# Source order on every engine, and weights' pieces issued three ahead from a flat list, in a two-layer decoder trunk

## The chip, the core and the metric

The kernel runs on one core of one Trainium2 chip. The core has engines that run their own instruction queues side by side: TensorE (PE) multiplies matrices and transposes, VectorE (DVE) and ScalarE (ACT) work elementwise, GpSimd (POOL) does what is left, and SyncE (SP) issues most transfers. An engine begins an instruction when the semaphores on which it waits have come. The metric is the device time of one execution in microseconds (us).

## What is computed

The input is x, 256 tokens of 2048 features in float32. Two layers follow each other, each a norm, one wide projection, a mixer, one output projection and a residual sum.

```python
def even_mixer(h, w_in, conv_w, w_out, pos):        # w_in: 2048 x 8192
    proj = h @ w_in
    q, k, v, g_ret, gate_b, gate_c, u, g_conv = jnp.split(proj, 8, axis=-1)
    ...
    o = retention_chunkwise(q, k, v.reshape(shp))
    ret_out = rms_norm_nogain(o).reshape(b, s, RET_WIDTH) * jax.nn.silu(g_ret)
    ...
    conv_out = gate_b * conv * jax.nn.silu(g_conv)
    return jnp.concatenate([ret_out, conv_out], axis=-1) @ w_out

def odd_mixer(h, w_in, q_norm_w, k_norm_w, sinks, w_out, pos):   # w_in: 2048 x 4608
    proj = h @ w_in
    q, k, v, gate = jnp.split(proj, [ATTN_WIDTH, ATTN_WIDTH + KV_WIDTH, ATTN_WIDTH + 2 * KV_WIDTH], axis=-1)
    q = rope(rms_norm(q.reshape(b, s, ATTN_Q_HEADS, ATTN_HEAD_DIM), q_norm_w), pos)
    k = rope(rms_norm(k.reshape(b, s, ATTN_KV_HEADS, ATTN_HEAD_DIM), k_norm_w), pos)
    o = swa_sinks(q, k, v, sinks).reshape(b, s, ATTN_WIDTH)
    return (o * jax.nn.silu(gate)) @ w_out
```

The attention of the odd layer has 32 query heads and 4 key heads of width 64, a window of 128 keys, and a learned sink per head in the softmax's divisor.

## The kernel before

**Products.** Every projection is computed as three products of rounded halves: x and w are each split into a high part and a remainder, and high times high, high times low and low times high are added. A projection goes in **chunks** of 512 output columns (`Chunk`, L126). A chunk has eight **pieces** of two k-tiles; the piece's weights are one transfer of 512 KB into `raw`, a copy on ACT that rounds them to `wh` (L165), and a subtraction on DVE that leaves `wl` (L166). These three are called the **split** (L157). `raw`, `wh` and `wl` have five buffers each. A piece's twelve matmuls (L143) go into two PSUM tiles, one for each half of the tokens (t = 0 and 1). Transfers, copies and subtractions are named for the chunk: `whog_3` is the rounded piece 3 of a gate chunk, `wloq_6` the remainder of piece 6 of a query chunk.

**Stages.** Layer 0 has sixteen chunks (names `e`), then four for its output projection (`eo`). The odd layer has nine: keys and values (`kv`), then q0, g0, q1, g1, q2, g2, q3, g3, where q is a chunk of eight query heads and g the gate of the same heads; then four chunks of output projection (`oo`). `stage` (L169) runs the first two chunks of a stage in turns, six pieces of the first, six of the second, two and two; the rest run one by one. When a chunk ends, its `done` function reads its PSUM tiles: `kv` (L516), `queries` (L566) or `gate` (L556).

**Side work.** What follows a chunk is partly put into generators in `pending`, and `feed` (L132) takes one step of them behind each piece (L136). `keys_values` (L525) scales and splits the keys, then transposes them on PE into two buffers of the pool `tp`, from which ACT copies them to kT (L551). `attention` (L589) runs through two chunks: it transposes the split queries (qt, L598, copied to q1T), computes scores for two heads at a time, masks them (L612 to L621), takes the shift and the sink (L625 to L636), the exponentials (L641), the divisor (L646), multiplies the gate with it (`scale_gate`, L654), transposes probabilities (pt) and the gate (gt, L665), computes values (ov, L697) and gates them (`gated`, L699). `finish` (L747) splits the result into the activations a2h and a2l of the last projection. `queries` needs, for each half of the tokens, a Square on ACT, a string of steps on DVE (a reduction, a product, two half products, a sum and a short step), and two copies qs on ACT.

**Order.** The program is written as one thread of calls, but the framework orders each engine's queue when it builds the program: an instruction may be moved ahead of others that stand earlier in the source, where its buffers are free. Splits have been moved up to five pieces ahead of their matmuls in this way, as far as the five buffers go.

Of the kernel before, what the change touches and what calls it, by code (L numbers as in the profile page):

```python
# [8 lines left out]
F32 = mybir.dt.float32  # L9
F32R = mybir.dt.float32r  # L10
AF = mybir.ActivationFunctionType
ALU = mybir.AluOpType
# [3 lines left out]
P = 128  # L16
# [4 lines left out]
N = 512  # L21
PK = 2
NP = KT // PK
# [7 lines left out]
EVEN_ORDER = [4, 0, 2, 6, 5, 1, 3, 7, 10, 12, 14, 8, 11, 13, 15, 9]  # L31

ODD_COLS = [2048, 0, 2560, 512, 3072, 1024, 3584, 1536, 4096]
ODD_KIND = [("kv", 0)] + [(k, i) for i in range(4) for k in ("q", "g")]

RAW_BUFS, HL_BUFS, W2_BUFS, WARM, LAST = 5, 5, 5, 2, 3


C_ID = 0
# [14 lines left out]
S_END = S_SINK + 32  # L54


@with_exitstack
def hybrid_kernel(
    ctx: ExitStack,
# [9 lines left out]
    const1: bass.AP,  # L69
    out: bass.AP,  # L70
):
    nc = tc.nc

    cp = ctx.enter_context(tc.tile_pool(name="cp", bufs=1))
    wp = ctx.enter_context(tc.tile_pool(name="wp", bufs=1))
# [14 lines left out]
    def f32(a):  # L90
        return a.bitcast(F32)

    class Act:


        def __init__(self, name):
            self.name, self.groups = name, []
# [15 lines left out]
    def step(n=1):  # L113
        while n and pending:
            try:
                next(pending[0])
                n -= 1
            except StopIteration:
                pending.popleft()

    def drain():
        while pending:
            step()


    class Chunk:  # L126
# [5 lines left out]
        def feed(self, lo, hi, steps=1, fine=False, late=False):  # L132

            for pc in range(lo, hi):
                self.products(pc, *self.split(pc, fine), late=late)
                step(steps)  # L136

        def products(self, pc, wh, wl, ts=range(T), late=False):

            def product(k, t, a, w):  # L140
                kt = pc * PK + k
                self.n[t] += 1
                nc.tensor.matmul(  # L143
                    self.ps[t], self.act(kt)[a][:, t * P : (t + 1) * P], w[:, k * N : (k + 1) * N],
                    start=self.n[t] == 1, stop=self.n[t] == 3 * KT,
                )

            for a, w in ((0, wh), (1, wh), (0, wl)) if late else ():
                for k in range(PK):
                    for t in ts:  # L150
                        product(k, t, a, w)
            for k in range(0 if late else PK):
                for t in ts:
                    for a, w in ((0, wh), (0, wl), (1, wh)):
                        product(k, t, a, w)

        def split(self, pc, fine=False):  # L157
            nm = f"{self.name}_{pc}"
            raw = wp.tile([P, PK * N], F32, tag="raw", name=f"w{nm}", bufs=RAW_BUFS)
            wh = wp.tile([P, PK * N], F32R, tag="wh", name=f"wh{nm}", bufs=HL_BUFS)  # L160
            wl = wp.tile([P, PK * N], F32R, tag="wl", name=f"wl{nm}", bufs=HL_BUFS)
            for k in range(PK if fine else 1):
                ws = slice(k * N, (k + 1) * N) if fine else slice(0, PK * N)
                nc.sync.dma_start(out=raw[:, ws], in_=self.w[self.c, pc, :, ws])
                nc.scalar.activation(wh[:, ws], raw[:, ws], AF.Copy)  # L165
                nc.vector.tensor_tensor(out=wl[:, ws], in0=raw[:, ws], in1=f32(wh[:, ws]), op=ALU.subtract)  # L166
            return wh, wl

    def stage(chunks, done):  # L169

        q = 3 * NP // 4
        a, b = Chunk(*chunks[0]), Chunk(*chunks[1])
        a.feed(0, q)
        b.feed(0, q)
        drain()
        a.feed(q, NP)
        done(0, a.ps)
        b.feed(q, NP)
        done(1, b.ps)
        for n in range(2, len(chunks)):  # L180
            c = Chunk(*chunks[n])
            c.feed(0, NP)
            done(n, c.ps)


    act0 = Act("a0")
# [25 lines left out]
            if g == 0 and lo == 0:  # L212
                ch0.feed(0, 1, fine=True, late=True)

    ch0 = Chunk("e0", w0, 0, act0)
    for g in range(KT // 4):
        load_act0(g)
        ch0.feed(max(1, 4 * g // PK), 4 * (g + 1) // PK, late=g < 2)
# [9 lines left out]
    with tc.tile_pool(name="e", bufs=1) as ep, tc.tile_pool(name="e2", bufs=2) as ep2:  # L228
# [5 lines left out]
        def load_x(t):  # L234
            nc.sync.dma_start(out=x[:, t, :], in_=xr[:, t, :])
            for c in range(4):
                junk = tw.tile([P, N], F32, tag="w2", name=f"jk{t}{c}")
                nc.scalar.activation(
                    junk, x[:, t, c * N : (c + 1) * N], AF.Square, accum_out=ssx[:, t, c : c + 1]
                )  # L240

        def stats():
            ss0 = cp.tile([P, T], F32, tag="ss0", name="ss0")
            nc.vector.tensor_reduce(out=ss0, in_=ssx, axis=AX.X, op=ALU.add)
            r = rsqrt_mean("n0", ss0, D, T)
            nc.vector.tensor_copy(r0, r)

        def load_tables():
            nc.sync.dma_start(out=cst0[:, :E_MASK], in_=const0[:, :E_MASK])
            for t in range(T):  # L250
                rt = cst0[:, E_ROPE0 + t * 512 : E_ROPE0 + (t + 1) * 512]
                nc.vector.tensor_scalar(out=rt, in0=rt, scalar1=r0[:, t : t + 1], scalar2=None, op0=ALU.mult)
# [121 lines left out]
        def even_done(n, ps):  # L374
            kind, i = EVEN_ORDER[n] // 2, EVEN_ORDER[n] % 2
            if kind in (0, 1):
                dst = ep.tile([P, 4, S], F32, tag="qk"[kind], name=f"{'qk'[kind]}T{i}")
                rope_pair(f"{kind}{i}", ps, dst)
                keep[kind] = dst
            elif kind in (2, 3, 5, 7):  # L380
                dst = ep.tile([P, T, N], F32, tag={2: "v", 3: "g", 5: "v", 7: "g"}[kind], name=f"e{kind}{i}")
                for t in range(T):
                    nc.scalar.activation(
                        dst[:, t, :], ps[t], AF.Silu if kind in (3, 7) else AF.Copy, scale=r0[:, t : t + 1]
                    )
                keep[kind] = dst
                if kind == 3:
                    pending.append(retention(i, keep[0], keep[1], keep[2], keep[3]))
            else:
                dst = ep.tile([P, T, N], F32, tag="q" if kind == 6 else "k", name=f"e{kind}{i}")  # L390
                for t in range(T):
                    nc.vector.scalar_tensor_tensor(
                        out=dst[:, t, :], in0=ps[t], scalar=r0[:, t : t + 1],
                        in1=keep[5 if kind == 6 else 7][:, t, :], op0=ALU.mult, op1=ALU.mult,
                    )
                keep[kind] = dst
                if kind == 4:
                    pending.append(conv(i, keep[6], keep[4]))

        for n, c in enumerate(EVEN_ORDER):  # L400
            if n == 0:
                continue
            ch = Chunk(f"e{c}", w0, n, act0)
            if n == 1:
                ch.feed(0, 1)
                load_x(0)
                ch.feed(1, 3)
                load_x(1)
                ch.feed(3, 5)
                stats()  # L410
                even_done(0, ch0.ps)
                load_tables()
                ch.feed(5, 6)
                nc.sync.dma_start(out=cst, in_=const1)
                nc.vector.tensor_copy(identr, ident)
                ch.feed(6, NP)
                nc.sync.dma_start(out=cst0[:, E_MASK:], in_=const0[:, E_MASK:])
            else:
                ch.feed(0, NP)
            even_done(n, ch.ps)  # L420
# [14 lines left out]
        def eo_turn(c):  # L435
# [15 lines left out]
            if c == 3:  # L451
# [3 lines left out]
                nc.vector.tensor_scalar(out=r1h, in0=r, scalar1=0.5, scalar2=None, op0=ALU.mult)  # L455

        stage([(f"eo{c}", w1, c, cact) for c in range(4)], eo_done)


    op = ctx.enter_context(tc.tile_pool(name="o", bufs=1))  # L460
# [126 lines left out]
    late = deque()  # L587
# [197 lines left out]
    def odd_done(n, ps):  # L785
# [5 lines left out]
        else:  # L791
            gate(i, ps)

    stage([(f"o{k}{i}", w2, n, act1) for n, (k, i) in enumerate(ODD_KIND)], odd_done)

    def oo_done(c, ps):
        for t in range(T):
            y = work(f"y{c}{t}", [P, N])
            nc.vector.tensor_tensor(out=y, in0=ps[t], in1=x[:, t, c * N : (c + 1) * N], op=ALU.add)
            nc.sync.dma_start(out=out[t * P : (t + 1) * P, c * N : (c + 1) * N], in_=y)  # L800

    stage([(f"oo{c}", w3, c, act2) for c in range(3)], oo_done)


    last = Chunk("oo3", w3, 3, act2)
    last.feed(0, NP - LAST)
    parts = [last.split(pc) for pc in range(NP - LAST, NP)]
    for t in range(T):
        for i, (wh, wl) in enumerate(parts):
            last.products(NP - LAST + i, wh, wl, (t,))  # L810
# [1 line left out]
        for c in range(1 + t):  # L812
            n = slice(c * N // (1 + t), (c + 1) * N // (1 + t))
# [84 lines left out]
```

## Time and profile before

| what | us |
|---|---|
| median of three runs | 803.32 (802.72 to 804.95) |
| the profiled execution | 804.01 |
| its span | 802.3 |
| outside the span | 1.7 |
| mean granted TensorE clock | 1.00 |
| memory traffic over the span | 183 GB/s |

The span is the time from the first to the last recorded instruction of the profiled execution. In the profile's rows, numbers on names are left out, so that `whog` stands for every piece of every gate chunk. A row of the timeline has the start, the duration, the engine, the line, the operation, its output and inputs, their sizes, a count, and in brackets the idle time ahead of it with what ended that. A row of the waits has who waited, for whom, the total, the number of times and the longest.

### The profile page before, as it was taken

To read this page: it belongs to the slowest core of one execution; us is meant where nothing else is said; L and a number is where in the kernel's file an instruction comes from. 1 tells how busy PE (TensorE), PEld (TensorE's weight loads), DVE (VectorE), ACT (ScalarE), POOL (GpSimd) and SP (SyncE) were. 2 spreads that over 40 slices of the span, in tenths; PEclk is the share of its full clock that TensorE was granted. 3 is DMA by queue.
4 is the path that set the end of the run, shared out by engine and by line. 5 is a ranking of instruction groups with operands and counts; after the bars stand their busy time and mean duration, and the time that the engine had idled before them with its cause. 6 is when DMAs were issued, how large, how long until landed. Compare 5 with 4: busy or idle time off the path is not lost.

```text
span 802.3 us, 10004 instructions
## 1 busy us (share of the span) xinstructions
PE 791.9 (99%) x3660; PEld 654.1 (82%) x3660; DVE 501.7 (63%) x742; ACT 419.5 (52%) x665; POOL 62.4 (8%) x61
## 2 busy tenths in 40 slices
PE   8999999999999999999999999999999999999998
PEld 6888888888888888888888888888878788788886
DVE  6566454664545475445856664877977977777651
ACT  6753434443444434443445443758658678586431
POOL 0000000000000000000000000420500601401000
PEclk9999999999999999999999999999999999999999
DMA  8966645555455655555555555462474454445750
GB/s 310 398 226 229 207 134 185 183 188 197 138 184 190 203 184 183 186 200 192 172 194 176 184 184 193 132 210 84 166 221 132 134 184 157 147 143 174 231 171 26
DMA packets 41088, 147.09 MB, mean 183 GB/s; under 512 B 4560, under 2 KB 4944, under 8 KB 40784
## 3 DMA queue, kind: packets, MB, share of 16 engines
q1 hardware_dynamic: 40752, 146.23, 54.5%
q8 instruction: 28, 0.46, 0.2%
q10 hardware_dynamic: 288, 0.24, 0.2%
q14 instruction: 20, 0.16, 0.1%
HBM read 144.36 MB, written 2.10 MB: 183 GB/s over the span
## 4 chain that ended last, share of the span: by engine, by line
PE 89%; DVE 4%; POOL 3%; issue 2%; ACT 1%; DMA 1%; DVEq 0%; ACTq 0%; POOLq 0%
PE pse L143 44%; PE psoo L143 11%; PE pseo L143 11%; PE psoq L143 10%; PE psog L143 3%; PE psokv L143 3%; POOL rq L225 2%; DVE wlog L166 1%; POOL qs L583 1%; PE pt L674 1%; DVE og L707 1%; DMA sml<-in_small 1%; PE qt L598 1%; PE s L606 0%; DVE og L709 0%
## 5 line engine op out<-in xcount | busy, mean ns | idle before, releaser
L166 DVE TENSOR_TENSOR wle<-we,whe 128x1024 fp32r<-128x1024 f32 (+1 forms) x129 | 156.3, 1217 | 148.6 <-ACT whe L165 148.3
L165 ACT ACTIVATE whe<-we 128x1024 fp32r<-128x1024 f32 (+1 forms) x129 | 135.6, 1052 | 173.9 <-PE pse L143 159.2
L143 PE MATMUL pse<-whe,a0h 128*128 128x512 f32 x512 | 200.0, 396 | 1.3 <-ACT whe L165 1.3
L143 PE MATMUL pse<-whe,a0l 128*128 128x512 f32 x512 | 198.3, 391 | 0.0
L143 PE MATMUL pse<-wle,a0h 128*128 128x512 f32 x512 | 197.8, 390 | 0.0
L143 PEld LDWEIGHTS pse<-whe,a0h 128*128 128x128 f32 x512 | 96.5, 189 | 22.4 <-ACT whe L165 2.9
L143 PEld LDWEIGHTS pse<-whe,a0l 128*128 128x128 f32 x512 | 96.7, 189 | 20.6
L143 PEld LDWEIGHTS pse<-wle,a0h 128*128 128x128 f32 x512 | 96.7, 189 | 19.8
L165 ACT ACTIVATE wheo<-weo 128x1024 fp32r<-128x1024 f32 x32 | 33.9, 1061 | 48.3 <-PE pseo L143 32.7
L166 DVE TENSOR_TENSOR wloo<-woo,whoo 128x1024 fp32r<-128x1024 f32 x32 | 39.5, 1239 | 27.8 <-ACT whoo L165 27.7
L166 DVE TENSOR_TENSOR wleo<-weo,wheo 128x1024 fp32r<-128x1024 f32 x32 | 39.2, 1225 | 27.5 <-ACT wheo L165 27.5
L165 ACT ACTIVATE whoo<-woo 128x1024 fp32r<-128x1024 f32 x32 | 33.9, 1062 | 37.9 <-PE psoo L143 32.7
L166 DVE TENSOR_TENSOR wloq<-woq,whoq 128x1024 fp32r<-128x1024 f32 x32 | 40.0, 1252 | 21.0 <-ACT whoq L165 20.5
L143 PE MATMUL psog<-whog,a1h 128*128 128x512 f32 x128 | 51.0, 398 | 0.0
L143 PE MATMUL psoq<-whoq,a1h 128*128 128x512 f32 x128 | 50.8, 397 | 0.0
L143 PE MATMUL pseo<-wheo,c0h 128*128 128x512 f32 x128 | 50.8, 397 | 0.0
L143 PE MATMUL psog<-wlog,a1h 128*128 128x512 f32 x128 | 50.0, 391 | 0.5 <-DVE wlog L166 0.5
L165 ACT ACTIVATE whoq<-woq 128x1024 fp32r<-128x1024 f32 x32 | 33.9, 1060 | 31.6 <-PE psoq L143 14.0
L143 PE MATMUL psoo<-whoo,a2h 128*128 128x512 f32 x128 | 50.3, 393 | 0.0
L143 PE MATMUL psoq<-wloq,a1h 128*128 128x512 f32 x128 | 50.0, 391 | 0.0
L143 PE MATMUL pseo<-wleo,c0h 128*128 128x512 f32 x128 | 50.0, 390 | 0.0
L143 PE MATMUL psoo<-whoo,a2l 128*128 128x512 f32 x128 | 50.0, 390 | 0.0
(182 smaller groups left out, 1246.3 us busy)
## 6 DMA issues: line engine op xcount, KB each, us to landing
we<-in_w SPq DMA_DIRECT2D x127, 512.0 KB, 3.3
weo<-in_w SPq DMA_DIRECT2D x32, 512.0 KB, 3.2
woq<-in_w SPq DMA_DIRECT2D x32, 512.0 KB, 4.2
wog<-in_w SPq DMA_DIRECT2D x32, 512.0 KB, 3.3
woo<-in_w SPq DMA_DIRECT2D x32, 512.0 KB, 4.2
wokv<-in_w SPq DMA_DIRECT2D x8, 512.0 KB, 3.2
x<-in_xr SPq DMA_DIRECT2D x2, 1024.0 KB, 9.5
out_y<-y SPq DMA_DIRECT2D x7, 256.0 KB, 4.5
```

What stands on the lines that cost most here:

```text
L143: nc.tensor.matmul(self.ps[t], self.act(kt)[a][:, t * P : (t + 1) * P], w[:, k * N : (k + 1) * N], start=self.n[t] == 1, stop=self.n[t] == ...
L165: nc.scalar.activation(wh[:, ws], raw[:, ws], AF.Copy)
L166: nc.vector.tensor_tensor(out=wl[:, ws], in0=raw[:, ws], in1=f32(wh[:, ws]), op=ALU.subtract)
L225: nc.gpsimd.tensor_tensor(out=r, in0=v, in1=mhalf[:, :width], op=ALU.pow)
L583: nc.gpsimd.tensor_tensor(out=q[:, :, 1, :], in0=aj, in1=f32(q[:, :, 0, :]), op=ALU.subtract)
L598: nc.tensor.transpose(tr[:, h, :], qs[j][:, h].rearrange("p a d -> p (a d)"), identr)
L674: nc.tensor.transpose(tr[:, h, :], pr[j][:, h, t, :], ident)
L707: nc.vector.tensor_tensor(out=og[half[e], :, ts], in0=o[half[e], :, e, :], in1=sh[half[e]], op=ALU.add)
```

## The change

Two things are changed. First, every instruction of the five engines goes through a wrapper (`Engines`, `InOrder`) that asks the framework to keep it in program order, so that each engine's queue is the source's order. Second, the pieces of all chunks are put on a flat list `plan` in the order in which they are used, and `piece` issues splits explicitly: before the matmuls of piece i come the splits of all pieces up to i + 3 that haven't been made yet. During the first chunk the number ahead is 0. `split` itself is the same, but is now a function of the plan's names.

```diff
+AHEAD = 3
...
+class InOrder:
...
+    def __getattr__(self, name):
+        f = getattr(self._engine, name)
+        def issue(*args, **kwargs):
+            ins = f(*args, **kwargs)
+            self._tc.keep_in_program_order(ins)
+            return ins
+        return issue
...
-    nc = tc.nc
+    nc = Engines(tc)
...
             for pc in range(lo, hi):
-                self.products(pc, *self.split(pc, fine), late=late)
+                self.products(pc, *self.piece(pc, fine), late=late)
                 step(steps)
...
+        def piece(self, pc, fine=False, ahead=None):
+            i = plan.index((self.name, pc))
+            while len(made) <= min(i + (ahead if ahead is not None else look[0]), len(plan) - 1):
+                name, nxt = plan[len(made)]
+                made.append(split(name, nxt, fine))
+            return made[i]
...
+    plan, made, look = [], [], [0]
+    source = {}
+    def schedule(name, w, c, pieces):
+        source[name] = (w, c)
+        plan.extend((name, pc) for pc in pieces)
...
+    for n, c in enumerate(EVEN_ORDER):
+        schedule(f"e{c}", w0, n, range(NP))
+    schedule_stage([f"eo{c}" for c in range(4)], w1, 4)
+    schedule_stage([f"o{k}{i}" for k, i in ODD_KIND], w2, len(ODD_KIND))
+    schedule_stage([f"oo{c}" for c in range(3)], w3, 3)
+    schedule("oo3", w3, 3, range(NP))
...
             ch = Chunk(f"e{c}", w0, n, act0)
+            look[0] = AHEAD
...
-    parts = [last.split(pc) for pc in range(NP - LAST, NP)]
+    parts = [last.piece(pc) for pc in range(NP - LAST, NP)]
```

What that does to the queues is seen on ACT. In the rows of the changed kernel, the line is always that of the wrapper. The number behind a name only tells instances apart.

The first place is the end of chunk q0, where `queries(0)` has its Squares (sqq) and copies (qs), and kT are the copies of the transposed keys. Before:

```order
L496 ACTIVATE sqq_3913<-psoq_0_3536,r_2815 128x512
L165 ACTIVATE whog_4_4058<-wog_4_4057 128x1024
L165 ACTIVATE whog_5_4088<-wog_5_4087 128x1024
L496 ACTIVATE sqq_3933<-psoq_1_3537,r_2815 128x512
L551 ACTIVATE kT<-kt_3973 128x4x128
L551 ACTIVATE kT<-kt_3979 128x4x128
L582 ACTIVATE qs_3927<-aq_3917 128x4x64
L582 ACTIVATE qs_3930<-aq_3917 128x4x64
L165 ACTIVATE whog_6_4118<-wog_6_4117 128x1024
L551 ACTIVATE kT<-kt_4003 128x4x128
L551 ACTIVATE kT<-kt_4009 128x4x128
```

Now:

```order
L68 ACTIVATE sqq_3931<-psoq_0_3554,r_2833 128x512
L68 ACTIVATE qs_3945<-aq_3935 128x4x64
L68 ACTIVATE qs_3948<-aq_3935 128x4x64
L68 ACTIVATE sqq_3951<-psoq_1_3555,r_2833 128x512
L68 ACTIVATE qs_3965<-aq_3955 128x4x64
L68 ACTIVATE qs_3968<-aq_3955 128x4x64
L68 ACTIVATE whog_3_3974<-wog_3_3973 128x1024
L68 ACTIVATE kT<-kt_3991 128x4x128
L68 ACTIVATE kT<-kt_3997 128x4x128
L68 ACTIVATE whog_4_4004<-wog_4_4003 128x1024
L68 ACTIVATE kT<-kt_4021 128x4x128
L68 ACTIVATE kT<-kt_4027 128x4x128
```

All of `queries(0)` and the split of g0's piece 3 now stand ahead of the first kT copies; before, two splits and two kT copies ran between its parts.

The second place is the softmax of attention group 0 during chunk q1: pr,den are the exponentials, es the sink's, pr<-s the copies of scores, ph the copy of the first transposed probabilities. Before:

```order
L165 ACTIVATE whoq_6_4412<-woq_6_4411 128x1024
L636 ACT_TABLE_LOAD
L636 ACTIVATE es_4211<-es_4211 128x8
L611 ACTIVATE pr_4237<-s_4238 128x2x128
L619 ACTIVATE pr_4237<-s_4239 128x2x128
L641 ACTIVATE pr_4154,den_4212<-pr_4154,nm_4210,rr_3912 128x128 x4
L611 ACTIVATE pr_4237<-s_4275 128x2x128
L619 ACTIVATE pr_4237<-s_4276 128x2x128
L641 ACTIVATE pr_4154,den_4212<-pr_4154,nm_4210,rr_3912 128x128 x4
L678 ACTIVATE ph_4330<-pt_4325 128x512
L636 ACTIVATE es_4291<-es_4291 128x8
```

Now:

```order
L68 ACTIVATE whoq_4_4237<-woq_4_4236 128x1024
L68 ACTIVATE pr_4255<-s_4256 128x2x128
L68 ACTIVATE pr_4255<-s_4257 128x2x128
L68 ACTIVATE pr_4172,den_4230<-pr_4172,nm_4228,rr_3930 128x128 x4
L68 ACTIVATE whoq_5_4276<-woq_5_4275 128x1024
L68 ACTIVATE pr_4255<-s_4293 128x2x128
L68 ACTIVATE pr_4255<-s_4294 128x2x128
L68 ACTIVATE es_4309<-es_4309 128x8
L68 ACTIVATE pr_4172,den_4230<-pr_4172,nm_4228,rr_3930 128x128 x4
L68 ACTIVATE whoq_6_4324<-woq_6_4323 128x1024
L68 ACTIVATE ph_4348<-pt_4343 128x512
```

Before, the splits up to q1's piece 6 were done ahead of the exponentials and piece 7 came behind this stretch; now the splits of pieces 4, 5 and 6 stand between them.

The third place is the end of chunk q1, where the values of group 0 (sh), its result (a2h), and `queries(1)` come together. Before:

```order
L678 ACTIVATE ph_4481<-pt_4476 128x512
L496 ACTIVATE sqq_4490<-psoq_0_4175,r_2815 128x512
L165 ACTIVATE whog_5_4660<-wog_5_4659 128x1024
L749 ACTIVATE a2h_4033<-og_4323 128x512
L496 ACTIVATE sqq_4510<-psoq_1_4176,r_2815 128x512
L165 ACTIVATE whog_6_4690<-wog_6_4689 128x1024
L582 ACTIVATE qs_4504<-aq_4494 128x4x64
L582 ACTIVATE qs_4507<-aq_4494 128x4x64
L705 ACTIVATE sh_4553<-ov_4550 64x256 x2
L582 ACTIVATE qs_4524<-aq_4514 128x4x64
L582 ACTIVATE qs_4527<-aq_4514 128x4x64
L165 ACTIVATE whog_7_4710<-wog_7_4709 128x1024
```

Now:

```order
L68 ACTIVATE sh_4479<-ov_4447 64x256 x2
L68 ACTIVATE a2h_4051<-og_4341 128x512
L68 ACTIVATE gT_4492<-gt_4487 128x512
L68 ACTIVATE ph_4499<-pt_4494 128x512
L68 ACTIVATE sqq_4508<-psoq_0_4193,r_2833 128x512
L68 ACTIVATE qs_4522<-aq_4512 128x4x64
L68 ACTIVATE qs_4525<-aq_4512 128x4x64
L68 ACTIVATE sqq_4528<-psoq_1_4194,r_2833 128x512
L68 ACTIVATE qs_4542<-aq_4532 128x4x64
L68 ACTIVATE qs_4545<-aq_4532 128x4x64
L68 ACTIVATE whog_3_4551<-wog_3_4550 128x1024
```

Before, the splits of g1's pieces 3 to 6 were spread before and among these rows; now piece 3 stands behind all of them. On PE and SP the rows stand nearly as before, and DVE's queue follows the same source order as ACT's.

More of the change, by code (lines that the diff above doesn't have):

```diff
@@ L54, with __init__ @@
 S_END = S_SINK + 32
+class InOrder:
+    def __init__(self, tc, engine):
+        self._tc, self._engine = tc, engine
+    def __getattr__(self, name):
[5 more added lines that the diff above has]
+        return issue
+class Engines:
+    def __init__(self, tc):
+        for e in ("tensor", "vector", "scalar", "gpsimd", "sync"):
+            setattr(self, e, InOrder(tc, getattr(tc.nc, e)))
 @with_exitstack
@@ L155, in products @@
                         product(k, t, a, w)
[L157 to L167, printed above, removed]
+    plan, made, look = [], [], [0]
@@ new lines, in hybrid_kernel, with split @@
+    source = {}
+    def schedule(name, w, c, pieces):
+        source[name] = (w, c)
+        plan.extend((name, pc) for pc in pieces)
+    def split(name, pc, fine=False):
+        w, c = source[name]
+        nm = f"{name}_{pc}"
+        raw = wp.tile([P, PK * N], F32, tag="raw", name=f"w{nm}", bufs=RAW_BUFS)
+        wh = wp.tile([P, PK * N], F32R, tag="wh", name=f"wh{nm}", bufs=HL_BUFS)
+        wl = wp.tile([P, PK * N], F32R, tag="wl", name=f"wl{nm}", bufs=HL_BUFS)
+        for k in range(PK if fine else 1):
+            ws = slice(k * N, (k + 1) * N) if fine else slice(0, PK * N)
+            nc.sync.dma_start(out=raw[:, ws], in_=w[c, pc, :, ws])
+            nc.scalar.activation(wh[:, ws], raw[:, ws], AF.Copy)
+            nc.vector.tensor_tensor(out=wl[:, ws], in0=raw[:, ws], in1=f32(wh[:, ws]), op=ALU.subtract)
+        return wh, wl
@@ new lines, in hybrid_kernel, with schedule_stage @@
+    Q = 3 * NP // 4
+    def schedule_stage(names, w, whole):
+        a, b = names[:2]
+        schedule(a, w, 0, range(Q))
+        schedule(b, w, 1, range(Q))
+        schedule(a, w, 0, range(Q, NP))
+        schedule(b, w, 1, range(Q, NP))
+        for c, name in enumerate(names[2:whole], 2):
+            schedule(name, w, c, range(NP))
+    for n, c in enumerate(EVEN_ORDER):
+        schedule(f"e{c}", w0, n, range(NP))
+    schedule_stage([f"eo{c}" for c in range(4)], w1, 4)
+    schedule_stage([f"o{k}{i}" for k, i in ODD_KIND], w2, len(ODD_KIND))
@@ L169, in stage @@
+    schedule_stage([f"oo{c}" for c in range(3)], w3, 3)
+    schedule("oo3", w3, 3, range(NP))
     def stage(chunks, done):
-        q = 3 * NP // 4
+        q = Q
         a, b = Chunk(*chunks[0]), Chunk(*chunks[1])
@@ L213, in load_act0 @@
                 ch0.feed(0, 1, fine=True, late=True)
-    ch0 = Chunk("e0", w0, 0, act0)
+    ch0 = Chunk(f"e{EVEN_ORDER[0]}", w0, 0, act0)
     for g in range(KT // 4):
```

## The prediction

> **What bounds the kernel now.** I read the page's busy shares first, then its slices and the chain, and then the waits of PE alone.
>
> ```profile
> PE 791.9 (99%) x3660; PEld 654.1 (82%) x3660; DVE 501.7 (63%) x742; ACT 419.5 (52%) x665; POOL 62.4 (8%) x61
> DVE  6566454664545475445856664877977977777651
> ACT  6753434443444434443445443758658678586431
> 81.71 19.10 PE pse L143 x84
> PE qt L598 <- ACT q1T L599: 3.2, 3, 1.1
> PE warm L195 <- DVE zero L192: 1.6, 1, 1.6
> PE pse L143 <- ACT whe L165: 1.3, 1, 1.3
> PE psog L143 <- DVE wlog L166: 0.5, 1, 0.5
> ```
>
> The first three lines are of the page, the fourth is a step of the chain, the last four are all waits that PE has. PE is busy 99% of the span; 84 matmuls in 19.10 us make .227 us for one and **2.73 us for a piece** of twelve. PE waits only 6.6 us, 2.9 of them at the start. So the change can hardly win: at most 3.2 + .5 us, plus scraps. It loses wherever a split or a copy reaches PE late. The places for that are the slices where DVE stands at 7 to 9 tenths, from 500 us on: the odd layer. DVE and ACT are not full there, but in a fixed order their idle time can no longer be used by whatever is ready.
>
> **Layer 0, eo and oo: nothing.** Three pieces ahead are 3 x 2.73 = 8.2 us of cover for PE.
>
> ```profile
> woo<-in_w SPq DMA_DIRECT2D x32, 512.0 KB, 4.2
> L165 ACT ACTIVATE whoq<-woq 128x1024 fp32r<-128x1024 f32 x32 | 33.9, 1060 | 31.6 <-PE psoq L143 14.0
> L166 DVE TENSOR_TENSOR wloq<-woq,whoq 128x1024 fp32r<-128x1024 f32 x32 | 40.0, 1252 | 21.0 <-ACT whoq L165 20.5
> 51.95 0.69 DVE L263 TENSOR_TENSOR ra<-pse,cst 128x512 f32<-128x512 f32 x1 [4.26 <-PE pse L143]
> ```
>
> A transfer takes 4.2 us, its copy 1.06 and its subtraction 1.25: 6.5 us, and 7.5 where an output is issued 1 us ahead of it on SP (the oo stage). Both are below 8.2. A rotary string on DVE holds six steps of about the last row's size, 4 us, and a split ahead of it or among them; at some 5.2 us it stays below the cover. The convolutions' strings come closest, and I keep 0 to 1 us for each of two of them and of three oo chunks, taking 0.
>
> **The kv and q0 boundary: +9.1 and +2.2.** PE's second pair of kt transpositions needs the two buffers that ACT's first pair of kT copies frees. Before, these copies ran ahead of the qs copies; now both Squares, all four qs and whog_3 of queries(0) stand ahead of them on ACT, and behind all of kv() too.
>
> ```profile
> 506.08 0.47 ACT L496 ACTIVATE sqk<-psokv,r 128x256 f32<-128x256 f32 x1 [0.98 <-PE psokv L143]
> 506.59 0.42 DVE L497 TENSOR_REDUCE ssk<-sqk 128x4 f32<-128x256 f32 x1 [0.23 <-ACT sqk L496]
> 512.71 0.68 DVE L537 TENSOR_TENSOR kl<-ak,kh 128x512 fp32r<-128x512 f32 x1
> 514.25 0.41 DVE L544 TENSOR_TENSOR vs<-scratch,vs 128x256 fp32r<-128x256 f32 x1
> 513.38 0.67 ACT L496 ACTIVATE sqq<-psoq,r 128x512 f32<-128x512 f32 x1
> 514.59 0.67 DVE L497 TENSOR_REDUCE ssq<-sqq 128x8 f32<-128x512 f32 x1
> 515.78 0.74 DVE L509 TENSOR_TENSOR bq<-psoq,cst 128x256 f32<-128x256 f32 x2
> 517.65 0.68 DVE L513 TENSOR_TENSOR aq<-aq,bq 128x512 f32<-128x512 f32 x1
> 518.36 0.72 ACT L582 ACTIVATE qs<-aq 128x256 fp32r<-128x256 f32 x2 [0.82 <-DVE aq L513]
> 516.46 1.08 ACT L551 ACTIVATE kT<-kt 128x512 fp32r<-128x512 f32 x2
> 518.20 0.46 PE L550 MATMUL kt<-identr,kh 128*128 128x128 f32 x4
> 525.25 0.50 PE L143 MATMUL psog<-wlog,a1h 128*128 128x512 f32 x1 [0.47 <-DVE wlog L166]
> ```
>
> In the new order, on the clock of the trace (a row's duration holds about .07 us that the next one on its engine overlaps): the k string of one half, Square .45 and then five short steps on DVE like its .42 reduction, takes 1.6 us and stands twice, with a scratch copy (.45) between that waits for the sums: 510.2. Then whog_1 511.2, wlog_1 512.4, the scaling, kh and kl of both halves 516.0, wlog_2 517.5, three vs 518.5. Of queries, one half is reduction, product, two half products, sum: .60 + .60 + .66 + .60, with a short step 2.55: DVE at 521.0; qs .73 and the second Square .65: 522.4; the second string 524.9; qs .73: 525.7; whog_3 1.0: 526.6; one kT copy .5: 527.1. PE arrives at 518.2, so it waits 8.9 and .2 more for the second buffer, **9.1**. Bounds: DVE's work in that stretch without a single wait on ACT is about 14 us from 506.6, then the last qs, whog_3 and kT, 522.8, a wait of 4.6; 25 handoffs between engines at .06 more each (the gap 506.55 to 506.59 is .04) give 10.6.
>
> ```profile
> 6.68 2.07 PE L143 MATMUL pse<-whe,a0h 128*128 128x512 f32 x4 [1.35 <-ACT whe L165]
> 11.61 1.09 PE L143 MATMUL pse<-whe,a0h 128*128 128x512 f32 x4
> 6.68:11.60 4.92, 4.92 (x12) 3.88 (x13) 4.33 (x8) 4.42 (x9) 0.00 (x0) 1.00 1.03 389
> ```
>
> After the start's idle time the first twelve matmuls take 4.93 us (6.68 to 11.61) instead of 2.73, though the granted clock reads 1.00 in that window. I charge the same **2.2** once, behind the 9 us of idle PE; bounds 0 to 2.2. [...]
>
> **The gate's transposition in each of four attention groups: +2.9 each.** PE's gt needs gv scaled by the divisor of the first four heads. Now the splits of pieces 3 to 6 stand between the steps of the softmax, on ACT and on DVE.
>
> ```profile
> 537.02 1.37 ACT L560 ACTIVATE gv<-psog,r1h 128x512 f32<-128x512 f32 x2 [0.98 <-PE psog L143]
> 543.39 0.42 DVE L612 TENSOR_TENSOR pr<-s,pr 128x256 f32<-128x256 f32 x1
> 545.41 0.16 DVE L635 TENSOR_TENSOR es<-sml,mx 128x8 f32<-128x8 f32 x1
> 544.62 1.06 ACT L165 ACTIVATE whoq<-woq 128x1024 fp32r<-128x1024 f32 x1 [1.85 <-PE psoq L143]
> 547.63 0.49 ACT L641 ACTIVATE pr<-pr,nm,rr 128x128 f32<-128x128 f32 x1
> 553.43 0.68 DVE L656 TENSOR_TENSOR gv<-gv,den 128x512 f32<-128x512 f32 x1
> 555.20 0.60 PE L665 MATMUL gt<-cst,gv 128*128 128x128 f32 x4
> ```
>
> Before, gv was ready at 554.11 and PE came at 555.20. A group of masking with its shift takes DVE 2.15 (543.39 to 545.57), four exponentials 4 x .49 = 1.95. The new chain begins when ACT has copied the first scores (538.8): tanh pair 1.25, whoq_3 1.0, wloq_3 1.2, masking and shift 2.15, es .2: 544.6; whoq_4 1.0, two copies .55, four exponentials 1.95, whoq_5 1.0: 549.1; wloq_5 1.2, masking and shift 2.15, es .2, exponentials 1.95: 554.6; whoq_6 1.0 (the divisor lies beside it), wloq_6 1.2, pl .6, gv .7: 558.1. That is **2.9 us late**, 11.6 for four groups. Bounds: .7 if one split's 2.2 falls beside other work, 3.8 with 15 handoffs of .06.
>
> **The burst at the end of q1, q2 and q3: +3.0 each.** Before, four or five splits were made ahead of it; now whog_3 stands behind the whole of it.
>
> ```profile
> 565.46 0.39 PE L697 MATMUL ov<-ul,vs 128*128 128x512 f32 x1
> 566.52 0.77 ACT L705 ACTIVATE sh<-ov 64x256 f32<-64x256 f32 x2
> 569.16 0.68 DVE L709 TENSOR_TENSOR og<-og,gT 128x512 f32<-128x512 f32 x1
> 576.14 0.39 PE L143 MATMUL psog<-whog,a1h 128*128 128x512 f32 x1
> 570.00:625.00 55.00, 53.91 (x270) 44.93 (x269) 44.69 (x91) 39.33 (x87) 13.41 (x13) 1.00 0.50 159
> ```
>
> From the end of that ov (565.85, zero below): sh .8, with og's adds 1.25, og's product 1.9, then on ACT a2h, gT and ph 3.5, Square 4.1, pl on DVE 4.2; first string 6.7, qs 7.4, Square 8.0, second string 10.6, qs 11.3, whog_3 12.3, wlog_3 13.5. PE wants whog_3 at 10.3 (576.14) and wlog_3 .23 later: it waits 2.0 and then 1.0, **3.0**, or 9.0 for three. Bounds: 0 if DVE's 8.7 us from og on ran without a gap; 4.0 with 16 handoffs of .06. The last row says how much room there is: DVE is busy 44.7 of 55 us in this stage.
>
> **What goes.** The qt waits (3.2 for three) came from ACT held by a2h, which had been moved ahead of the q1T copies; in source order it stands behind them: -3.3 with the scraps. The wait of .47 on wlog vanishes in the longer one at kt: -.5. PE's and SP's orders are otherwise nearly the old ones.
>
> **Sum.** 9.1 + 2.2 + 11.6 + 9.0 - 3.8 = +28.1. The profiled execution took 804.01 (span 802.3 and 1.7 outside it), which gives 832.1; against the median of 803.32 the forecast is **831**.
>
> **Rivals.** (1) Only the largest wait and the bursts come: the gt chains hide, since PE comes to them late from small waits that I don't count: 803.3 + 9.1 + 2.2 + 9.0 - 3.8 = 820. For it: ACT idles 1.85 us ahead of a whoq there (the row at 544.62); against it: the chain is serial, so idle time doesn't shorten it. (2) The array falls cold after each of the seven 3 us waits as well: 7 x 2.2 = 15.4 more, 847. [...] (3) Faster: the cover is enough, because the strings on ACT and DVE overlap more than I let them. It decides at two points: whog_3 done within 10.3 us of the last ov, and the kT copy by 518.2. Then only the -3.8 stays, 799.5. Against it: qs waited .82 us for its aq already when nothing was pinned. (4) The order of PE and SP hardly moves, and all the rest hides: 803.
>
> **Chances.** The forecast with all three kinds of wait (823 to 841) .64, rival 1 .14, rival 2 .11, rival 3 .07, rival 4 .04. The range 814 to 848 takes in the first three. A measurement of this kernel can tell about .3%, 2.4 us, from no change: faster .07, same .04, slower .89.
>
> **What would show it.** In the profile after, PE's list of waits has kt behind ACT's kT once, near 9 us; gt behind DVE's gv four times near 3; psog behind wh and wl of piece 3, three times near 2 and 1; and no qt. Twelve matmuls behind the kt wait take near 4.9 us. Wrong would be: kt below 5 us, gt not in the list, or waits in layer 0 or the convolutions, which I cost at nothing.

## The result, and the profile after

The changed kernel takes **857.13 us** (median of four runs, 856.06 to 860.5) where the kernel before took 803.71 in the runs beside it: a ratio of 1.067, interval 1.064 to 1.071. It is slower, as forecast, but by 53 us and not by 28; the time lies above the range. The profiled execution took 856.06, with a span of 854.3 and a mean granted clock of .978 (before: 802.3 and 1.00).

First the lines of the page that answer to those of before: busy time by engine, the slices of DVE and ACT, and the granted clock by slices.

```profile
PE 809.1 (95%) x3660; PEld 663.1 (78%) x3660; DVE 503.0 (59%) x742; ACT 415.4 (49%) x665; POOL 59.4 (7%) x61
...
DVE  6566355554544665457565647466766766766453
ACT  7653353443534253425344435474674674675232
...
PEclk9999999999999999999999997999999999999999
```

Then all of PE's waits of .3 us or more in sum (who waited, for whom, total, times, longest).

```profile
PE gt L68 <- DVE gv L68: 12.2, 4, 3.1
PE kt L68 <- ACT kT L68: 9.6, 1, 9.6
PE psog L68 <- ACT whog L68: 8.3, 3, 2.8
PE psoo L68 <- ACT whoo L68: 2.5, 1, 2.5
PE psog L68 <- DVE wlog L68: 2.3, 3, 0.8
PE warm L68 <- DVE zero L68: 1.6, 1, 1.6
PE s L68 <- DVE pr L68: 1.3, 4, 0.3
PE pse L68 <- ACT whe L68: 1.2, 2, 0.7
PE x1t L68 <- DVE x L68: 1.0, 1, 1.0
PE psoo L68 <- DVE wloo L68: 0.8, 1, 0.8
PE pse L68 <- DVE wle L68: 0.3, 1, 0.3
PE pseo L68 <- DVE wleo L68: 0.3, 1, 0.3
```

DVE and ACT do as much work as before (503.0 against 501.7 us, 415.4 against 419.5); the fullest slices of DVE are emptier, since the same work is stretched. Two numbers make the whole difference of the spans, 52.0 us. **PE's waits** sum to 41.4 us where they were 6.6: 34.8 more. **PE's busy time** is 809.1 where it was 791.9, with the same 3660 matmuls: 17.2 more. Waits were what the forecast was made of. Slower matmuls were one term of 2.2 us in it.

Where the busy time comes from is seen behind any of the long waits. The first group's gt, in PE's timeline (start, duration), and then two windows of the same stretch (length, then busy time of PE, PEld, DVE, ACT and POOL, the granted clock, and the share and rate of the transfers):

```profile
571.12 0.94 PE L68 MATMUL gt<-cst,gv 128*128 128x128 f32 x4 [3.08 <-DVE gv L68]
571.71 0.78 PE L68 MATMUL psoq<-whoq,a1h 128*128 128x512 f32 x1
572.29 0.63 PE L68 MATMUL psoq<-wloq,a1h 128*128 128x512 f32 x1
...
574.42 0.53 PE L68 MATMUL psoq<-whoq,a1h 128*128 128x512 f32 x1
574.79 0.39 PE L68 MATMUL psoq<-wloq,a1h 128*128 128x512 f32 x1
```

```profile
570.50:575.00 4.50, 3.88 (x12) 3.27 (x13) 2.50 (x5) 4.50 (x14) 1.84 (x2) 0.62 0.60 177
576.00:580.00 4.00, 4.00 (x22) 3.30 (x20) 3.43 (x5) 1.82 (x3) 0.00 (x0) 1.00 0.42 131
```

From 571.71 to 574.79 seven products start where thirteen would at .227 us each; that alone is 1.5 us, and the four transpositions take .94 where they took .60. The granted clock is .62 in the one window and 1.00 in the next. So a long wait of this kernel costs its own length and **about 1.7 us behind it**. The nine long stops of the list (kt, four gt, three on whog, one on whoo) make some 15 of the 17.2; the other 2 are not accounted for here.

At the boundary of kv and q0, ACT's timeline reads as the prediction laid it out: one half of the queries, the other, whog_3, and only then the first kT copies, for which PE waits.

```profile
523.05 0.72 ACT L68 ACTIVATE qs<-aq 128x256 fp32r<-128x256 f32 x2 [3.39 <-DVE aq L68]
523.68 0.67 ACT L68 ACTIVATE sqq<-psoq,r 128x512 f32<-128x512 f32 x1
527.09 0.72 ACT L68 ACTIVATE qs<-aq 128x256 fp32r<-128x256 f32 x2 [2.74 <-DVE aq L68]
527.71 1.04 ACT L68 ACTIVATE whog<-wog 128x1024 fp32r<-128x1024 f32 x1
528.66 1.07 ACT L68 ACTIVATE kT<-kt 128x512 fp32r<-128x512 f32 x2
529.29 0.75 PE L68 MATMUL kt<-identr,kh 128*128 128x128 f32 x4 [9.56 <-ACT kT L68]
```

ACT idles 3.4 and 2.7 us here with work behind it that was ready: that is what pinning does. The brackets on qs name DVE, which makes each half's string in turn.

The wait that I didn't foresee is in the output projection, where SP, ACT and DVE meet:

```profile
802.45 2.47 DVE L68 TENSOR_TENSOR wloo<-woo,whoo 128x1024 fp32r<-128x1024 f32 x2 [5.75 <-ACT whoo L68]
804.83 1.28 DVE L68 TENSOR_TENSOR y<-psoo,x 128x512 f32<-128x512 f32 x2
805.54 0.94 SPq L68 DMA_DIRECT2D out_y<-y  x2
806.58 9.87 SPq L68 DMA_DIRECT2D woo<-in_w  x8
810.97 1.06 ACT L68 ACTIVATE whoo<-woo 128x1024 fp32r<-128x1024 f32 x1 [7.30 <-DMA woo<-in_w]
812.08 0.50 PE L68 MATMUL psoo<-whoo,a2h 128*128 128x512 f32 x1 [2.51 <-ACT whoo L68]
```

Two subtractions stand ahead of the sum y on DVE, out_y stands behind y on SP, the next weights stand behind out_y, and PE waits for their copy.

### The profile page after: what moved, and what is told of

It is laid out like the page before. It is cut to its first block, busy times and chain, and to the rows that moved or that the text cites. A ratio compares the mean times of both kernels' runs of the same rounds, so it can differ in the third digit from the quotient of the medians.

```text
span 854.3 us, 9986 instructions
## 1 busy us (share of the span) xinstructions
PE 809.1 (95%) x3660; PEld 663.1 (78%) x3660; DVE 503.0 (59%) x742; ACT 415.4 (49%) x665; POOL 59.4 (7%) x61
## 4 chain that ended last, share of the span: by engine, by line
PE 76%; DVE 12%; ACT 7%; issue 2%; DMA 2%; SPq 0%; DVEq 0%; ACTq 0%
PE pse L68 40%; PE pseo L68 9%; PE psog L68 8%; PE psoo L68 7%; PE psoq L68 5%; PE psokv L68 2%; ACT pr L68 2%; DVE pr L68 2%; DVE aq L68 1%; DMA woo<-in_w 1%; DVE wloq L68 1%; DVE wloo L68 1%; DVE mx L68 1%; DVE gv L68 1%; DVE ca L68 1%
## 5 line engine op out<-in xcount | busy, mean ns | idle before, releaser
L68 DVE TENSOR_TENSOR wle<-we,whe 128x1024 fp32r<-128x1024 f32 (+1 forms) x129 | 154.2, 1215 | 118.8 <-ACT whe L68 118.5
L68 ACT ACTIVATE whe<-we 128x1024 fp32r<-128x1024 f32 (+1 forms) x129 | 133.2, 1051 | 98.3 <-PE pse L68 92.9
L68 PE MATMUL psog<-whog,a1h 128*128 128x512 f32 x128 | 53.9, 421 | 8.3 <-ACT whog L68 8.3
L68 PE MATMUL psog<-wlog,a1h 128*128 128x512 f32 x128 | 52.8, 412 | 2.3 <-DVE wlog L68 2.3
L68 PE MATMUL psoq<-whoq,a1h 128*128 128x512 f32 x128 | 52.9, 413 | 0.0
L68 PE MATMUL psog<-whog,a1l 128*128 128x512 f32 x128 | 52.4, 409 | 0.0
L68 PE MATMUL psoo<-wloo,a2h 128*128 128x512 f32 x128 | 51.3, 401 | 0.8 <-DVE wloo L68 0.8
L68 PE MATMUL psoq<-wloq,a1h 128*128 128x512 f32 x128 | 51.8, 405 | 0.0
L68 PE MATMUL psoq<-whoq,a1l 128*128 128x512 f32 x128 | 51.5, 402 | 0.0
L68 PE MATMUL pseo<-wheo,c0l 128*128 128x512 f32 x128 | 49.8, 389 | 0.0
```

The costliest lines, as they stand in the source:

```text
L68: ins = f(*args, **kwargs)
```

## The experiments

Theory A is that the pinned order of ACT and DVE makes serial strings ahead of what PE waits for, and that PE's stop itself makes the matmuls behind it slow. Twelve kernels were run; the kernel before took 803.0 to 803.3 us beside them.

**The list without the pins.** All engines are ordered by the framework again; the list and the three pieces stay.

```diff
-    nc = Engines(tc)
+    nc = tc.nc
```

> The flat list with three pieces ahead stays, the pinning is undone on all five engines. Theory A (the pinned order of ACT and DVE makes serial strings in front of what PE waits for): the kt, gt and piece-3 waits are gone, 802 to 807 us. Rival B (three instead of up to five pieces ahead is what is missing): the waits on whog and whoo of piece 3 stay, 2 to 3 us each, and the time stays above 825.

Measured: **797.59 us** (five runs, 797.17 to 798.86), ratio .994, interval .9925 to .9956. It is faster than both kernels, and below the range I gave it. These are all its waits on PE:

```profile
PE warm L253 <- DVE zero L250: 1.5, 1, 1.5
PE pse L175 <- ACT whe L205: 1.4, 2, 0.9
```

Rival B falls: three pieces ahead are enough when the queues are free. The three qt waits and the one on wlog of the kernel before (3.2 and .5 us) are gone; ACT's a2h, which had held the q1T copies for 3.96 us, now waits 1.15. At the start, PE begins its third piece at 12.71 instead of 14.35. Together these are 5.3 of the 6.6 us by which the span is shorter; the rest I didn't trace, and which property of the list brings it was not tried. The 1.64 us at the start can't safely be put down to the list: how long the first products run slow differs between executions with the same start. The changed kernel and the one with later key transpositions (below) have the same instructions there, and their third pieces begin at 12.56 and 13.57.

**Four pieces ahead, all pinned.**

```diff
-AHEAD = 3
+AHEAD = 4
```

> Everything pinned, four pieces ahead instead of three (as many as five buffers allow). Theory A: the four waits on piece 3 (2.8 and .8 us each) fall by a piece's 2.7 us and lose their slow matmuls (1.7 us each), so about 17 us less, 839; the kt wait (9.6) and the four gt waits (3.05 each) stay as they are, since as many splits stand between the softmax steps. Rival B: the depth was the cause of all of them, and the time comes back below 815.

Measured: 836.47 us (ratio 1.042, 1.035 to 1.048), as theory A said. The waits on PE of 2 us or more in sum:

```profile
PE gt L68 <- DVE gv L68: 12.1, 4, 3.0
PE kt L68 <- ACT kT L68: 9.6, 1, 9.6
PE psog L68 <- DVE wlog L68: 2.3, 3, 0.8
```

The waits on whog are gone; kt and gt haven't moved by a tenth. Depth buys time only where the split stands behind one burst.

**One engine free.** The pins stay on PE, POOL and SP and on one of DVE and ACT.

```diff
-        for e in ("tensor", "vector", "scalar", "gpsimd", "sync"):
-            setattr(self, e, InOrder(tc, getattr(tc.nc, e)))
+        pinned = ("tensor", "vector", "gpsimd", "sync")
+        for e in ("tensor", "vector", "scalar", "gpsimd", "sync"):
+            eng = getattr(tc.nc, e)
+            setattr(self, e, InOrder(tc, eng) if e in pinned else eng)
```

> Pinned on PE, DVE, POOL and SP; ACT is free again. Theory A, with the strings made of alternate steps on ACT and DVE: kT copies and wh copies run where they are ready, so kt falls below 3 us, gt goes (its chain loses 4 us of whoq copies), and piece 3 waits less than 1 us for DVE's fixed string: 806 to 818. If DVE's fixed order alone makes the waits, little changes: above 840.

Measured with ACT free: 818.82 us (1.020, 1.016 to 1.024), just above the range. kt and gt are gone from the list, as expected; what is left there is DVE's fixed string, and it is dearer than I said in one place (4.1 us on wlog behind queries(0)), with the output projection's wait as before:

```profile
PE psog L68 <- DVE wlog L68: 7.1, 4, 4.1
PE psoo L68 <- ACT whoo L207: 2.8, 1, 2.8
```

With DVE free instead and ACT pinned ("scalar" in place of "vector"):

> Pinned on PE, ACT, POOL and SP; DVE is free again. Theory A: the kT copies and whog_3 still stand behind qs on ACT, so kt stays at 6 to 10 us and piece 3 at 1 to 2.8, while gt loses the DVE half of its splits and falls below 1.5: 825 to 842. If DVE's order alone makes the waits, 803 to 812.

Measured: 845.1 us (1.052, 1.048 to 1.057), 3 us above the range. kt falls to 8.7 only, and gt to 2.5 each instead of below 1.5; what gt waits for is now pl, not gv. The waits on whog grow to 3.5 each. So ACT's order is the dearer of the two: freeing it saves 38 us, freeing DVE 12.

With both free, and PE, POOL and SP pinned:

> Pinned on PE, POOL and SP alone; ACT and DVE are free. Theory A (only the pinned order of ACT and DVE costs): 795 to 800 as with nothing pinned. If the pinned SP or POOL queues cost something too: 802 or more.

Measured: 803.89 us (1.002, 1.000 to 1.003), above the 795 to 800 of theory A and within what I gave for a cost of pinned SP or POOL. But the waits that are left point to the pinned PE: none is in the odd layer, and two new ones are in the convolutions:

```profile
PE bt L68 <- DVE ca L425: 3.0, 2, 1.5
PE yt L68 <- DVE ca L415: 1.9, 2, 1.0
```

These 4.9 us stand in neither the free kernel nor the fully pinned one. The framework put DVE's steps where a free PE would have gone round them, and the pinned PE stood; that cause is read from the two lists, not tried.

**One split fewer in the softmax.** From piece 5 of a g chunk to piece 2 of the next q chunk four pieces are issued ahead, and three elsewhere, so that three splits and not four stand between the first scores and gt.

```diff
+                if look[0]:
+                    k, i = self.name[:2], self.name[2:]
+                    look[0] = 4 if (k == "og" and pc >= 5) or (k == "oq" and i != "0" and pc <= 2) or (self.name == "oo0" and pc <= 2) else AHEAD
                 self.products(pc, *self.piece(pc, fine), late=late)
```

> The changed kernel, but one split more is issued ahead from piece 5 of each g chunk to piece 2 of the next q chunk, so that three splits instead of four stand between the copies of the first scores and gt. Theory A (a serial chain over ACT and DVE): each gt wait falls by one split, 1.0 + 1.2 = 2.2, to about .8, and the slow matmuls after it go: 4 x (2.2 + 1.7) = 15.6 less, 839 to 844. If the splits lie beside the softmax steps and not in the chain: 855 to 859.

Measured: 843.91 us (1.051, 1.048 to 1.054), at the upper end of theory A's range.

```profile
PE gt L68 <- DVE gv L68: 5.9, 4, 1.5
```

gt falls from 3.05 to 1.5 each, less than the 2.2 I gave a split, and no matmul is slow behind any of the four. The splits do stand in the chain.

**The key transpositions three pieces later.**

```diff
         yield
+        yield
+        yield
+        yield
         for t in range(T):
             for i, src in enumerate(ks[t]):
```

> The changed kernel with the key transpositions three pieces later, so that PE no longer meets them behind piece 1 of g0. Theory A (ACT's whole queue is late behind queries(0), whog_3 with it): the kt wait is gone, but piece 3 of g0 waits 7 us for whog_3 and .8 for wlog_3: 852 to 857. If only the two transposition buffers were the trouble: 9.6 + 1.7 less, 844 to 847.

Measured: 858.98 us (1.070, 1.067 to 1.073). The kt wait is gone and its successor is where it was expected, behind queries(0):

```profile
PE gt L68 <- DVE gv L68: 24.2, 7, 5.1
PE psog L68 <- ACT whog L68: 6.5, 1, 6.5
```

But the time went 2 us past the expected 852 to 857: with everything three pieces later the second gt of a group waits too (seven waits now, up to 5.1). The two transposition buffers were not the trouble; the queue of ACT was.

**What makes the matmuls slow.** The first try put extra matmuls into the tile that gt overwrites.

```diff
             tr = tp.tile([P, 2, S], F32, tag="tp", name=f"gt{g}{j}")
+            if j == 0:
+                for _ in range(12):
+                    nc.tensor.matmul(tr.rearrange("p a s -> p (a s)"), kT[:, 0, 0, 0, :], kT[:, 0].rearrange("p t i q -> p (t i q)"), start=True, stop=True)
```

> The changed kernel with twelve extra matmuls on PE ahead of the gate's first transposition (gt) in each of the four groups, into the tile that gt then overwrites; 12 x .227 = 2.7 us of work in a place where PE waits 3.05. Theory A (the slow matmuls after a wait come from PE's idleness): the waits on gv fall to about .3, the some seven matmuls at .63 us after each go back to .39, and 4 x 1.7 = 7 us are saved in spite of more work: 848 to 852. Rival C (they are slow because of what else runs then, or because PE draws too much): the extra work brings nothing, 855 or more.

Measured: 863.73 us (1.076, 1.073 to 1.079). The time lies where I had put rival C, but it says nothing on either theory: the tile's buffer was itself not free, so that the extra matmuls waited 2.4 us for DVE's pl before they ran, and lengthened the path.

```profile
570.62 4.50 PE L68 MATMUL gt<-kT 128*128 128x512 f32 x12 [2.36 <-DVE pl L68]
```

The second try multiplies by a tile of zeros and adds to the running chunk's sums, which are always writable.

```diff
+    def dummies(n):
+        c = cur[0]
+        rhs = c.act.groups[0][0][:, 0:2, :].rearrange("p a s -> p (a s)")
+        for _ in range(n):
+            nc.tensor.matmul(c.ps[0], zr, rhs, start=False, stop=False)
...
+            if j == 0:
+                dummies(12)
             tr = tp.tile([P, 2, S], F32, tag="tp", name=f"gt{g}{j}")
```

> As e5, but the twelve extra matmuls multiply by zeros and add to the chunk's own sums, so that they wait for nothing and lie in PE's idle time ahead of gt. Theory A: the four gt waits shrink to .3 or .4 each and no matmul at .63 follows them; some 4 x 1.7 = 7 us less than the changed kernel, 849 to 852. Rival C (not PE's idleness): 855 to 859.

Measured: 853.58 us (1.062, 1.057 to 1.067), half of the expected gain, and between the ranges of the two theories. The gt waits shrink to .25 each and no matmul at .63 follows them. But the stops on whog and whoo that were left had 12 or 13 such matmuls behind them in three of four cases, 2.5 to 3 us, where all four had seven or eight.

So eight of the nine stops were filled: also 40 ahead of the second pair of key transpositions, and 11 and 3 in piece 3 of g1, g2 and g3.

> As e9, and extra matmuls also ahead of the second pair of key transpositions (40) and of the first two products of piece 3 of g1, g2, g3 (11 and 3): eight of the nine long waits are filled. Theory A: eight times 1.7 = 14 us less than the changed kernel, 841 to 846, though PE does 130 matmuls more and no wait is truly shorter. Rival C: 855 or more.

Measured: **843.21 us** (1.049, 1.044 to 1.053), 13.9 us less than the changed kernel, with 130 matmuls more on PE. Eight stops at 1.7 are 13.6. One window of 500 to 800 us, first of the changed kernel, then of this one (the granted clock is the third number from the end):

```profile
500.00:800.00 300.00, 266.38 (x1239) 218.67 (x1238) 198.72 (x392) 174.36 (x368) 54.89 (x50) 0.94 0.38 126
```

```profile
500.00:800.00 300.00, 293.75 (x1411) 240.31 (x1409) 201.95 (x397) 177.56 (x372) 54.97 (x50) 1.00 0.41 135
```

The clock is 1.00 instead of .94, and the eight matmuls at .63 that are left stand behind the one stop that was not filled. DVE, ACT and POOL do the same work in both, and transfers run at 126 and 135 GB/s. So the slow matmuls come from PE's own idleness; rival C falls.

**SP free.** All other engines are pinned.

> Everything pinned but SP. If the waits on whoo in the output projection (2.5 and .8 us) come from weights that stand behind out_y on SP, they go with the slow matmuls behind them: 5 us less than the changed kernel, 850 to 853. If they come from DVE's order alone (y behind two subtractions), they stay: 855 to 858.

Measured: 851.0 us (1.059, 1.053 to 1.065; two runs, 849.63 and 852.37). Both waits of the output projection are gone from the list, and 6 us with them. They are also gone with DVE free and SP pinned, the kernel that took 845.1: there the second y begins 4.07 us after DVE's last work, as soon as PE has finished the sums, and out_y still stands ahead of the weights on SP. So it takes both, the weights behind out_y and y behind two subtractions, and freeing either queue is enough.

**Nothing pinned, four pieces ahead.** The first two experiments' edits together.

> Nothing pinned, the list with four pieces ahead. PE has no waits left behind its start in e1, so depth can't give more: 796 to 799. If depth was still worth something: below 796.

Measured: 798.61 us (.995, .993 to .997). No different from three ahead.

## Why the prediction was wrong

The direction, the mechanism and its three kinds of place were right; **the step that failed is the slow clock**. Point by point:

- **kt, +9.1:** measured 9.6. The split of pieces 3 to 6 ahead of gt, +2.9 each: 3.05. Piece 3 behind the burst, +3.0: 2.8 and .8, together 3.5. These three terms came to 29.7 and measured 32.4. The kernels with four pieces ahead, with one split fewer and with ACT free show that each is what it was taken for.
- **What goes, -3.8:** the qt waits and the one on wlog are gone, as forecast.
- **The clock, +2.2, charged once "behind the 9 us of idle PE":** this is the term that was mis-sized. Behind kt it was right: the products there lost 1.66 us and the transpositions .41. But it is due behind all nine long stops, the shortest of them 2.51 us long (on whoo), about 1.7 us each, and PE's busy time rose by 17.2. My second rival had just this, at seven stops, 2.2 us each, and with a chance of .11; I held it down because the only slow rows I had were those of the start. Behind the eight shorter stops my 2.2 would have been too much. The granted clock of 1.00 that the forecast read beside the slow products of the start was no reading: that trace has no record of the clock before 11.2 us, about where the slow products end.
- **eo and oo, nothing, "0 to 1 us for each":** the output projection lost 3.3 us in one stop, and 1.7 behind it. The sum of 7.5 us that I held against the cover of 8.2 began at the end of the chunk. But y doesn't start there: it stands behind two subtractions on DVE, whose weights had themselves been issued behind the earlier out_y.
- **Small ones that I didn't count:** four waits of .3 at the scores, 1.0 at the transposition of x1, .3 twice in layer 0 and eo: together 2.9.

Added up in PE's waits: 32.4 + 3.3 + 2.9 - 3.7, and .1 less at the start, are the 34.8 measured; the forecast had 25.9. With 17.2 instead of 2.2 for slow matmuls, 52.0 instead of 28.1. Of the 24 us by which I was off, 15 are the clock, 6 the waits that I costed at nothing, and 3 the three terms, each of them right within a fifth.

## What to carry to other kernels

When every queue is pinned to source order, follow the string of handoffs between engines up to what the busiest engine waits for; depth of prefetch covers one burst, and it doesn't take a split out of a chain. When the busiest engine is TensorE, allow for slow matmuls behind its long stops (here, in the changed kernel, about 1.7 us behind each of nine of 2.5 to 9.6 us), and fill such a stop with harmless products if it can't be removed (here 13.9 us for eight). A change with two parts is worth measuring by parts: here the list alone is .6% faster than before, and the pins cost it 7%.

## What the hardware showed that I had not expected

Stops as short as 2.51 us (on whoo in the changed kernel, ending at 812.08) are followed by matmuls that start every .43 us instead of .227, but not always: with four pieces ahead, no matmul is slow behind the gt wait of 3.03 us that ends at 631.06, and with the key transpositions later there is none behind the one of 3.03 us that ends at 578.25. Behind the four gt waits of 1.5 us that one split fewer leaves there were none. How many follow varies, too: behind stops of 2.8 us on whog from 6 to 14 (1.5 to 3.0 us).

The traces show that the length alone doesn't settle it. In the changed kernel the granted clock falls to .50 nine times: for 10.24 us from 523.51 on, during and behind the kt wait, and for 3.41 us at each of the other eight long stops. From the start of one of these stretches to the start of the next it is 27.3, 37.5 or 47.8 us: 8, 11 or 14 times 3.41. With four pieces ahead, the first two gt waits end at 570.75 and at 631.06, and both are 3.0 us long; each row is one stretch of such a grid (start and end, length, then busy time of PE, PEld, DVE, ACT and POOL, the granted clock, and the share and rate of the transfers):

```profile
568.51:571.93 3.42, 1.19 (x8) 1.08 (x9) 2.51 (x4) 3.42 (x12) 0.00 (x0) 1.00 0.44 135
571.93:575.34 3.41, 3.41 (x10) 2.67 (x9) 1.95 (x6) 3.37 (x11) 1.84 (x2) 0.50 0.48 160
...
626.54:629.95 3.41, 1.49 (x9) 1.03 (x7) 2.00 (x5) 3.41 (x12) 0.00 (x0) 1.00 0.01 2
629.95:633.37 3.42, 2.31 (x12) 2.01 (x13) 2.50 (x4) 3.42 (x10) 1.02 (x1) 1.00 0.48 153
633.37:636.78 3.41, 3.41 (x16) 2.82 (x15) 1.95 (x5) 3.35 (x10) 0.82 (x2) 1.00 0.48 154
```

The first stop falls mostly into one stretch, in which PE is busy for 1.19 of 3.41 us, and the next stretch runs at .50. The second is split between two, with PE busy for 1.49 and 2.31, and the clock stays at 1.00. PE's busy time in a stretch doesn't settle it either. In the changed kernel the stop on whog that ends at 725.92 lies in two stretches, from 721.48 and from 724.90; PE is busy for 1.66 and 1.63 us of them, and the clock is 1.00 behind the first and .50 behind the second. So a stop near 3 us can be followed by slow matmuls or by none, and neither its length nor PE's busy time around it tells which here. No run moved a stop on purpose to test what does.
